# Splitting each chunk of feature weights into two halves, laid at two pairs of column offsets

## The chip, the cores and the metric

One core of one Trainium2 chip. The metric is the device time of one execution in microseconds (us). An execution on one core is measured a few times; the median is given. Beside it stands one execution taken with the profiler, from which all rows below come.

## The reference

One hybrid decoder layer on 256 tokens of width 1024, in float32:

```
u = rms_norm(h, attn_pre_norm);  q, k, v, x_lru, g_lru, gate_attn, gate_lru = split(u @ w_in)
attn   = causal attention, 8 heads of 128, rotary on 32 of the 128 dims of q and k
hl     = rg_lru(causal_conv4(x_lru));  r, i = sigmoid(block-diagonal 4 x (256 x 256))
merged = sigmoid(gate_attn) * (attn @ w_branch_attn) + sigmoid(gate_lru) * ((hl * gelu(g_lru)) @ w_branch_lru)
h = h + rms_norm(merged @ w_out)
h = h + rms_norm(relu(rms_norm(h) @ w_up)^2 @ w_down)
```

Seven products of 1024 x 1024 make `u @ w_in`, three more the branches and the output, four each the two parts of the feed-forward network.

## The kernel before

**Weights.** The weights are cut into 74 chunks of 128 x 2048 float32 (1 MB), numbered in the order of use: 0, 2, 4, 6 x_lru; 1, 3, 5, 7 v; 8 to 11 q; 12 to 15 k; 16 and 17 the gates of the recurrence (`rg`); 18 to 21 g_lru; 22 to 25 gate_attn; 26 to 29 gate_lru; 30 to 37 the branches; 38 to 41 the output; 42 to 57 up; 58 to 73 down. TensorE multiplies in fp32r, and a chunk is split in two for it: `hi` is the raw chunk cast to fp32r, and `lo` is raw minus `hi`. The activations are split alike (`xh`, `xl`), and a product is three matmuls (`three`, L179 to L182): hi·xh, hi·xl, lo·xh.

**Stages of a chunk.** SP loads the raw chunk (L92) into one of three buffers; ACT casts `hi` (L117), or DVE does for chunks 17 to 22 (L115, `HI_ON_VECTOR`); DVE subtracts `lo` (L118). `hi` and `lo` have three buffers each. `ahead(c)` issues the loads up to chunk c + 3 and the splits up to chunk c + 1 ahead of what follows it in the code; a split is issued at high priority, and a scheduler that goes by priorities then lays down the final order on each engine. The load of chunk c + 3 waits for the subtract of chunk c, since it takes its raw buffer; the cast of chunk c + 3 waits until PE has done with chunk c.

**A feature chunk.** In `feat_chunk` (L201) the output comes out as features on partitions, tokens on columns. A chunk holds 256 output features, as two halves o of 128, over 1024 inputs in eight blocks kb. PE goes through o, then kb, with three matmuls each, 48 in all; the stationary operand is a block of 128 x 128 of the weights, the moving one the activations of 128 x 256. In the chunk the columns lie as (kb, o, 128): the blocks that follow each other on PE are 256 columns apart. The two `rg` chunks (L337 on) use the same weights' layout, by groups g. The tiles of `hi` and `lo` are 64 columns wider than a chunk, and `OFFSET` shifts what lies in them, by c mod 3: `hi` and `lo` begin at columns (13, 16), (16, 13) or (13, 13). Chunk 0 has its own loop (`first_chunk`). The chunks of v, of the output (38 to 41), 42 and 43, and those of down go through other code, have no offsets and aren't touched.

**The rotation of the keys.** For chunks 12 to 15 DVE multiplies the sums by `rstd` into `kT` (L325), and POOL copies 32 rows of each chunk's result to `rot` by DMA (L326). Then DVE shuffles (L327), multiplies twice (L328, L329) and adds (L330), and POOL writes the 32 rows back into `kT` with four DMAs (L332). The scores of head 0, `s0` (L387, L388), read `kT`. The recurrence's product `it` (L361) runs on DVE in between.

Of the kernel before, what the change touches and what calls it, by code (L numbers as in the profile page):

```python
# [9 lines left out]
F32 = mybir.dt.float32  # L10
F32R = mybir.dt.float32r
AF = mybir.ActivationFunctionType
ALU = mybir.AluOpType
PSUM = bass.MemoryType.PSUM

P = 128
T = 256
D = 1024
KB = D // P
# [9 lines left out]
NCHUNK = 74  # L29


HI_ON_VECTOR = {c: 1.0 for c in range(17, 23)}


(P_W0, P_W1, P_W2, P_W3, P_CB, P_BA, P_BI, P_LAM, P_G1, P_G2) = range(0, 80, 8)
# [6 lines left out]

OFFSET = {c: ((13, 16), (16, 13), (13, 13))[c % 3] for c in (*range(0, 8, 2), *range(8, 38), *range(44, 58))}


@with_exitstack
def hybrid_layer(ctx: ExitStack, tc: tile.TileContext, head_d, x_d, w_d, cst_d, gp_d, out_d):
    nc = tc.nc  # L50
# [18 lines left out]
    def slot_tile(i, name, dt=F32, shape=(P, KB, T)):  # L69
        if i not in laid:  # L70
            laid.add(i)
            gap(slot, f"s{i}")
        return slot.tile(list(shape), dt, tag=f"s{i}", name=name)

    def mm_bank(name):
        return ps_mm.tile([P, 512], F32, tag="mm", name=name)
# [9 lines left out]
    raws, splits = {}, {}  # L86
# [8 lines left out]
    def weight_tiles(c):  # L95
        hi = whi_p.tile([P, 2048 + W_STEP], F32R, tag="whi", name=f"whi{c}")
        lo = wlo_p.tile([P, 2048 + W_STEP], F32R, tag="wlo", name=f"wlo{c}")
        h, l = OFFSET.get(c, (0, 0))
        return hi[:, h:h + 2048], lo[:, l:l + 2048]


# [2 lines left out]
    def split(c):  # L104
        raw, parts = raws.pop(c)
        if c in own_slots:
            hi, lo = (slot_tile(i, f"w{c}_{i}", F32R, (P, 2048)) for i in own_slots[c])
        else:
            hi, lo = weight_tiles(c)
        n = 2048 // parts  # L110
        for i in range(parts):
            s = slice(i * n, (i + 1) * n)
            k = i * n + int(n * HI_ON_VECTOR.get(c, 0))
            if k > i * n:
                nc.vector.tensor_copy(hi[:, i * n:k], raw[:, i * n:k])  # L115
            if k < (i + 1) * n:
                nc.scalar.copy(hi[:, k:(i + 1) * n], raw[:, k:(i + 1) * n])  # L117
            nc.vector.tensor_tensor(lo[:, s], raw[:, s], hi[:, s].bitcast(F32), ALU.subtract)  # L118
        splits[c] = (hi, lo)

    state = {"load": 0, "split": 0}
# [1 line left out]
    def ahead(c):  # L123

        while state["load"] < min(NCHUNK, c + 4):
            load(state["load"])
            state["load"] += 1
        while state["split"] < min(NCHUNK, c + 2):
            with tc.high_priority():
                split(state["split"])  # L130
            state["split"] += 1
# [47 lines left out]
    def three(out, wh, wl, xh, xl, start, stop):  # L179
        nc.tensor.matmul(out, wh, xh, start=start, stop=False)  # L180
        nc.tensor.matmul(out, wh, xl, start=False, stop=False)  # L181
        nc.tensor.matmul(out, wl, xh, start=False, stop=stop)  # L182

    def blocks(w):

        return w.rearrange("p (k o c) -> p k o c", k=KB, o=2)

    def of(x):
        return lambda kb: x[:, kb, :]

# [10 lines left out]
    def feat_chunk(c, xh, xl, urgent=False):  # L201

        ahead(c + 1)
        hi, lo = (blocks(w) for w in splits.pop(c))
        bank = mm_bank(f"mm{c}").rearrange("p (o t) -> p o t", o=2)
        for o in range(2):
            for kb in range(KB):
                three(bank[:, o, :], hi[:, kb, o, :], lo[:, kb, o, :], xh(kb), xl(kb),
                      kb == 0, kb == KB - 1)
        if not urgent:  # L210
            ahead(c + 2)
        return bank
# [51 lines left out]
    for j in range(4):  # L264
        s = slice(2 * j, 2 * j + 2)
# [71 lines left out]
    for c, dst, pb in ((C_RGA, rt, P_BA), (C_RGI, it, P_BI)):  # L337
        ahead(c + 1)
        hi, lo = splits.pop(c)
        hi = hi.rearrange("p (g k c) -> p g k c", g=4, k=2)  # L340
        lo = lo.rearrange("p (g k c) -> p g k c", g=4, k=2)
        for g in range(4):
            bank = mm_bank(f"rg{c}_{g}").rearrange("p (o t) -> p o t", o=2)
            for o in range(2):
                s = slice(o * P, (o + 1) * P)
                for k in range(2):
                    three(bank[:, o, :], hi[:, g, k, s], lo[:, g, k, s],
                          xch[:, 2 * g + k, :], xcl[:, 2 * g + k, :], k == 0, k == 1)
            for o in range(2):
                nc.scalar.activation(dst[:, 2 * g + o, :], bank[:, o, :], AF.Sigmoid,  # L350
                                     bias=pcol(pb, 2 * g + o))
# [83 lines left out]
    for kind, c0 in (("gL", C_GL), ("gA", C_GA), ("gelu", C_GEL)):  # L435
        for j in range(4):
            bank = feat_chunk(c0 + j, of(xgh), of(xgl))
            s = slice(2 * j, 2 * j + 2)
# [4 lines left out]
            else:  # L443
                g = tmp.tile([P, 2, T], F32, tag="g", name="g")
# [181 lines left out]
    for j in range(14):  # L626
        bank = feat_chunk(C_UP + j, lambda kb: u2h(kb, slice(0, T)), lambda kb: u2l(kb, slice(0, T)), True)
        o = 4 + 2 * j
# [4 lines left out]
        s = slice(o % 8, o % 8 + 2)  # L633
        hi = rrh[o // 8][:, s, :]
# [5 lines left out]
    parts = (halves, halves)  # L640
    norms = [TokenNorm("d", len(parts[b])) for b in range(2)]
    res = slot.tile([P, 2, D], F32, tag="s11", name="res")
    for b, i, acc in tok_products(C_DN, 16, lambda kb: (rrh[kb // 8][:, kb % 8, :], rrl[kb // 8][:, kb % 8, :]),
# [3 lines left out]
        s = parts[b][i]  # L647
# [7 lines left out]
def _rotary(np):  # L655

    inv = np.float32(500000.0) ** (-np.arange(0, 32, 2, dtype=np.float32) / np.float32(32))
    ang = (np.arange(T, dtype=np.float32)[:, None] * inv[None, :].astype(np.float32)).T
    cos = np.concatenate([np.cos(ang)] * 2)
    sin = np.concatenate([-np.sin(ang), np.sin(ang)])  # L660
    return np.tile(np.stack([cos, sin], axis=1), (4, 1, 1)).astype(np.float32)


def _pack(np, inp):

    def a(name):
        return np.asarray(inp[name])[0]

    def stat(w):
        k, n = w.shape  # L670
        w = w.reshape(k // P, P, n // 256, 256).transpose(2, 1, 0, 3)
        return [w.reshape(n // 256, P, 2048)]

    w_in = a("w_in")

    def halves(w):
        n = w.shape[1] // 512
        return w.reshape(2, 4, P, n, 512).transpose(3, 0, 2, 1, 4).reshape(2 * n, P, 2048)
# [12 lines left out]
    chunks += stat(w_in[:, 0:D])
    chunks += stat(w_in[:, D:2 * D])
    chunks += [rg(a("w_rg_a")), rg(a("w_rg_i"))]
    chunks += stat(w_in[:, 6 * D:7 * D])
    chunks += stat(w_in[:, 5 * D:6 * D])
    chunks += stat(w_in[:, 4 * D:5 * D])
    chunks += stat(a("w_branch_attn"))
    chunks += stat(a("w_branch_lru"))
    chunks += [mov(a("w_out"))]
    chunks += [halves(a("w_mlp_up")[:, 0:512])]  # L700
    chunks += stat(a("w_mlp_up")[:, 512:])
    chunks += [mov(a("w_mlp_down"))]
    w = np.concatenate(chunks, axis=0)
    w0, w = w[0].reshape(P, KB, 256), w[1:]

    rows = list(a("conv_w")) + [a(n) for n in ("conv_b", "b_rg_a", "b_rg_i", "lru_lambda",
                                               "attn_pre_norm", "mlp_pre_norm")]
    par = np.stack(rows).reshape(10, KB, P).transpose(2, 0, 1).reshape(P, NPAR)
    x = a("x")
    xw = np.concatenate([x.T.reshape(KB, P, T).transpose(1, 0, 2), w0], axis=2).reshape(P, KB * 512)  # L710
    return {
        "head": np.concatenate([par, xw], axis=1),
        "x": x,
        "w": w,
        "cst": _rotary(np),
        "gp": np.stack([a("attn_post_norm"), a("mlp_post_norm")]),
    }
# [19 lines left out]
```

## Time and profile before

| | us |
|---|---|
| runs | 437.81, 438.69, 438.76 (median 438.69) |
| the profiled execution | 438.56 |
| its span, first to last instruction | 436.8 |
| PE busy (matmuls) | 424.4 (97%) |
| DVE busy | 292.4 (67%) |
| ACT busy | 238.5 (55%) |
| share of PE in the chain that ended last | 91% |

The span is 1.8 us shorter than the profiled execution's time. Busy time of PE is that of overlapping matmuls: each is shown with its own length, 0.28 us for 256 columns, while the next starts 0.11 us after it. So how fast PE works is read from the starts of matmuls, not from their lengths, and whether it waits from the idle time ahead of one.

### The profile page before, as it was taken

The page shows a single profiled execution, that of the slowest core. Times are in us where ns is not written, and L with a number is a line of the kernel's source. Part 1 is how long each engine was busy: PE and PEld are TensorE (multiplying, and loading weights), DVE is VectorE, ACT ScalarE, POOL GpSimd, SP SyncE. Part 2 cuts the span into 40 slices and gives each one's busy share as a digit, 9 for nine tenths or more (in the row PEclk, how much of TensorE's full clock was granted, in tenths as well). Part 3 has the DMA queues.
Part 4 walks back from the last instruction along what each step waited for, and adds up shares of the span by engine and source line. Part 5 has one row for each costly group of instructions (what it writes and reads, how often), then busy time and mean ns, then how long its engine had stood idle before and what let it go on. Part 6 is the DMA issues. An engine that isn't in the chain of part 4 may idle for free.

```text
span 436.8 us, 7246 instructions
## 1 busy us (share of the span) xinstructions
PE 424.4 (97%) x3044; PEld 397.6 (91%) x3044; DVE 292.4 (67%) x353; ACT 238.5 (55%) x326; POOL 21.0 (5%) x48
## 2 busy tenths in 40 slices
PE   6989999999999999999999999999999999999994
PEld 6979999999999999999998879999999888888883
DVE  5649975779998646996689565666666644444434
ACT  7585663319996676663556474555555533333321
POOL 1000054202100000000000000000000000000000
PEclk9999999999999999999999999999999999999999
DMA  8969555665644355555567703455555555555102
GB/s 285 391 231 337 170 195 209 218 224 194 227 147 168 122 194 197 189 194 194 192 206 294 272 0 131 169 196 195 203 185 192 193 193 195 191 197 190 83 2 96
DMA packets 14576, 83.61 MB, mean 191 GB/s; under 512 B 1808, under 2 KB 2576, under 8 KB 5456
## 3 DMA queue, kind: packets, MB, share of 16 engines
q1 hardware_dynamic: 13520, 80.39, 50.8%
q0 software_dynamic: 736, 2.36, 1.7%
q8 instruction: 24, 0.39, 0.4%
q10 hardware_dynamic: 288, 0.39, 0.3%
q14 instruction: 8, 0.07, 0.0%
HBM read 81.04 MB, written 1.05 MB: 188 GB/s over the span
## 4 chain that ended last, share of the span: by engine, by line
PE 91%; DMA 5%; ACT 1%; DVE 1%; issue 0%; SPq 0%; DVEq 0%
PE mm L182 18%; PE mm L180 18%; PE mm L181 18%; PE acc L497 8%; PE acc L496 8%; PE acc L495 8%; DMA x_tok<-in_x_dram 3%; DMA wraw<-in_w_dram 1%; DMA xw_a<-in_head_dram 1%; PE up L602 1%; PE up L604 1%; PE rg L182 1%; PE v L234 1%; PE v L233 1%; PE up L603 1%; PE v L235 1%
## 5 line engine op out<-in xcount | busy, mean ns | idle before, releaser
L118 DVE TENSOR_TENSOR wlo<-wraw,whi 128x2048 fp32r<-128x2048 f32 (+2 forms) x78 | 163.5, 2100 | 84.7 <-ACT whi L117 84.7
L117 ACT CAST whi<-wraw 128x2048 fp32r<-128x2048 f32 (+2 forms) x72 | 125.2, 1741 | 90.9 <-PE acc L497 46.2
L180 PE MATMUL mm<-xgh,whi 128*128 128x256 f32 x384 | 108.2, 285 | 4.2 <-ACT xgh L171 4.2
L182 PE MATMUL mm<-xgh,wlo 128*128 128x256 f32 x384 | 107.1, 280 | 1.6 <-DVE wlo L118 1.6
L181 PE MATMUL mm<-xgl,whi 128*128 128x256 f32 x384 | 107.3, 280 | 0.0
L180 PEld LDWEIGHTS mm<-xgh,whi 128*128 128x128 f32 x384 | 72.4, 190 | 4.5 <-ACT xgh L171 4.2
L182 PEld LDWEIGHTS mm<-xgh,wlo 128*128 128x128 f32 x384 | 73.0, 190 | 1.8 <-DVE wlo L118 1.8
L181 PEld LDWEIGHTS mm<-xgl,whi 128*128 128x128 f32 x384 | 72.9, 190 | 0.5
L180 PE MATMUL mm<-u,whi 128*128 128x256 f32 x224 | 62.0, 277 | 0.0
L182 PE MATMUL mm<-u,wlo 128*128 128x256 f32 x224 | 62.0, 277 | 0.0
L181 PE MATMUL mm<-u,whi 128*128 128x256 f32 x224 | 62.0, 277 | 0.0
L495 PE MATMUL acc<-whi,rrh 128*128 128x512 f32 x128 | 49.8, 389 | 0.0
L496 PE MATMUL acc<-wlo,rrh 128*128 128x512 f32 x128 | 49.8, 389 | 0.0
L497 PE MATMUL acc<-whi,rrl 128*128 128x512 f32 x128 | 49.8, 389 | 0.0
L180 PEld LDWEIGHTS mm<-u,whi 128*128 128x128 f32 x224 | 42.1, 188 | 0.0
L181 PEld LDWEIGHTS mm<-u,whi 128*128 128x128 f32 x224 | 42.1, 188 | 0.0
L182 PEld LDWEIGHTS mm<-u,wlo 128*128 128x128 f32 x224 | 42.1, 188 | 0.0
L495 PEld LDWEIGHTS acc<-whi,rrh 128*128 128x128 f32 x128 | 24.0, 188 | 5.0
L496 PEld LDWEIGHTS acc<-wlo,rrh 128*128 128x128 f32 x128 | 24.0, 188 | 5.0
L497 PEld LDWEIGHTS acc<-whi,rrl 128*128 128x128 f32 x128 | 24.0, 188 | 4.9
L637 ACT CAST rrh<-rv 128x512 fp32r<-128x512 f32 x14 | 8.7, 621 | 34.7 <-DVE rv L636 34.7
L182 PE MATMUL mm<-lrh,wlo 128*128 128x256 f32 x64 | 17.7, 276 | 0.0
(197 smaller groups left out, 667.1 us busy)
## 6 DMA issues: line engine op xcount, KB each, us to landing
wraw<-in_w_dram SPq DMA_DIRECT2D x70, 1024.0 KB, 4.8
wraw<-in_w_dram SPq DMA_DIRECT2D x8, 256.0 KB, 5.8
xw_a<-in_head_dram SPq DMA_DIRECT2D x4, 256.0 KB, 4.5
wraw<-in_w_dram SPq DMA_DIRECT2D x2, 512.0 KB, 7.5
x_tok<-in_x_dram SPq DMA_DIRECT2D x1, 1024.0 KB, 11.3
gp<-in_gp_dram POOLq DMA_DIRECT2D x1, 1024.0 KB, 7.0
xw_b<-in_head_dram SPq DMA_DIRECT2D x3, 256.0 KB, 5.1
out_dram<-res ACTq DMA_DIRECT2D x2, 192.0 KB, 2.0
```

The costliest lines, as they stand in the source:

```text
L117: nc.scalar.copy(hi[:, k:(i + 1) * n], raw[:, k:(i + 1) * n])
L118: nc.vector.tensor_tensor(lo[:, s], raw[:, s], hi[:, s].bitcast(F32), ALU.subtract)
L180: nc.tensor.matmul(out, wh, xh, start=start, stop=False)
L181: nc.tensor.matmul(out, wh, xl, start=False, stop=False)
L182: nc.tensor.matmul(out, wl, xh, start=False, stop=stop)
L233: nc.tensor.matmul(banks[b], xgh[:, kb, s], hi[:, k, :], start=kb == 0, stop=False)
L234: nc.tensor.matmul(banks[b], xgh[:, kb, s], lo[:, k, :], start=False, stop=False)
L235: nc.tensor.matmul(banks[b], xgl[:, kb, s], hi[:, k, :], start=False, stop=kb == KB - 1)
L495: nc.tensor.matmul(out, xh[:, s], hi[:, hs], start=first, stop=False)
L496: nc.tensor.matmul(out, xh[:, s], lo[:, hs], start=False, stop=False)
L497: nc.tensor.matmul(out, xl[:, s], hi[:, hs], start=False, stop=last)
L637: nc.scalar.copy(hi, v)
```

## The change

The host lays out a chunk of features as (o, kb, 128) instead of (kb, o, 128), so that each half o is 1024 columns in one piece, and its blocks are 128 columns apart. In the tile the two halves are placed separately: `hi` at columns 13 and 1040, `lo` at 1040 and 13. Against the start of 1024 columns these are the pairs (13, 16) and (16, 13) for `hi` and `lo` of half 0 and half 1, though half 0 of `lo` lies in the upper part of its tile. Each half of a feature chunk is cast and subtracted by itself, 128 x 1024, and PE waits for each by itself. This holds for the `rg` chunks too. Chunk 0 has the offsets (13, 13) instead of (13, 16). Sizes and places of the tiles are as before.

```
+FEATURES = {*range(2, 8, 2), *range(8, 38), *range(44, 58)}
+HALF = 1024
+PLACE_HI = (13, HALF + 16)
+PLACE_LO = (HALF + 16, 13)
...
-        h, l = OFFSET.get(c, (0, 0))
+        if c in FEATURES:
+            return tuple([w[:, at:at + HALF] for at in places] for w, places in ((hi, PLACE_HI), (lo, PLACE_LO)))
+        h, l = (PLACE_HI[0], PLACE_LO[1]) if c == 0 else (0, 0)
         return hi[:, h:h + 2048], lo[:, l:l + 2048]
...
+        if c in FEATURES:
+            parts = max(parts, 2)
         n = 2048 // parts
         for i in range(parts):
...
+            r, s, h, l = raw[:, i * n:(i + 1) * n], slice(i * n, (i + 1) * n), hi, lo
+            if c in FEATURES:
+                s = slice(i * n % HALF, i * n % HALF + n)
+                h, l = hi[i * n // HALF], lo[i * n // HALF]
+            if c in HI_ON_VECTOR:
+                nc.vector.tensor_copy(h[:, s], r)
+            else:
+                nc.scalar.copy(h[:, s], r)
+            nc.vector.tensor_tensor(l[:, s], r, h[:, s].bitcast(F32), ALU.subtract)
...
         for o in range(2):
             for kb in range(KB):
-                three(bank[:, o, :], hi[:, kb, o, :], lo[:, kb, o, :], xh(kb), xl(kb),
-                      kb == 0, kb == KB - 1)
+                s = slice(kb * P, (kb + 1) * P)
+                three(bank[:, o, :], hi[o][:, s], lo[o][:, s], xh(kb), xl(kb), kb == 0, kb == KB - 1)
...
-        w = w.reshape(k // P, P, n // 256, 256).transpose(2, 1, 0, 3)
+        w = w.reshape(k // P, P, n // 256, 2, P).transpose(2, 1, 3, 0, 4)
```

The lines move: L117 and L118 become L126 and L127, L115 becomes L124, L180 to L182 become L189 to L191, the rotation's L325 to L332 become L330 to L337, the scores' L387 and L388 become L391 and L392, and `it`'s L361 becomes L365.

The scheduler's order moves with it, at three places that matter here. The numbers at the ends of names are those of buffers, and the number behind `whi`, `wlo`, `wraw` and `mm` is the chunk's.

The first is DVE around chunk 4. Before:

```order
L118 TENSOR_TENSOR wlo3_243<-wraw3_108,whi3_242 128x1024 x2
L253 RECIPROCAL rstd_t_361<-rstd_t_361 128x2
L118 TENSOR_TENSOR wlo4_275<-wraw4_218,whi4_274 128x2048
L259 COPY rstd_367<-bc_364 128x256
L270 TENSOR_TENSOR xlp_159<-mm0_0_168,rstd_367 128x256
L270 TENSOR_TENSOR xlp_159<-mm0_1_169,rstd_367 128x256
L118 TENSOR_TENSOR wlo5_330<-wraw5_220,whi5_329 128x2048
L277 SCALAR_TENSOR_TENSOR xc_161<-xlp_159,head_87,xc_161 128x256 x2
```

The same place of DVE after:

```order
L127 TENSOR_TENSOR wlo3_243<-wraw3_108,whi3_242 128x1024 x2
L258 RECIPROCAL rstd_t_363<-rstd_t_363 128x2
L127 TENSOR_TENSOR wlo4_275<-wraw4_218,whi4_274 128x1024 x2
L264 COPY rstd_369<-bc_366 128x256
L275 TENSOR_TENSOR xlp_159<-mm0_0_168,rstd_369 128x256
L275 TENSOR_TENSOR xlp_159<-mm0_1_169,rstd_369 128x256
L277 TENSOR_TENSOR xlp_159<-mm2_280,rstd_369 128x2x256
L127 TENSOR_TENSOR wlo5_332<-wraw5_220,whi5_331 128x2048
```

Chunk 4's subtract is in two pieces, and the product of chunk 2's sums into `xlp` has moved ahead of chunk 5's subtract.

The second is DVE at the rotation of the keys. Before:

```order
L118 TENSOR_TENSOR wlo18_1093<-wraw18_976,whi18_1092 128x2048
L327 STREAM_SHUFFLE rot_626<-rot_626 128x512
L328 TENSOR_TENSOR rot_626<-rot_626 128x512
L115 CAST whi19_1170<-wraw19_1033 128x2048
L329 TENSOR_TENSOR rot_626<-rot_626 128x512
L118 TENSOR_TENSOR wlo19_1171<-wraw19_1033,whi19_1170 128x2048
L330 TENSOR_TENSOR rot_626<-rot_626 128x512
L361 TENSOR_TENSOR it_1107<-it_1107,xc_161 128x1024
L115 CAST whi20_1244<-wraw20_1090 128x2048
L361 TENSOR_TENSOR it_1107<-it_1107,xc_161 128x1024
L118 TENSOR_TENSOR wlo20_1245<-wraw20_1090,whi20_1244 128x2048
```

The same place of DVE after:

```order
L127 TENSOR_TENSOR wlo18_1117<-wraw18_996,whi18_1116 128x1024 x2
L330 TENSOR_TENSOR kT_633<-mm15_1065,rstd_369 128x512
L124 CAST whi19_1196<-wraw19_1055 128x1024 x2
L127 TENSOR_TENSOR wlo19_1197<-wraw19_1055,whi19_1196 128x1024 x2
L332 STREAM_SHUFFLE rot_634<-rot_634 128x512
L333 TENSOR_TENSOR rot_634<-rot_634 128x512
L334 TENSOR_TENSOR rot_634<-rot_634 128x512
L365 TENSOR_TENSOR it_1133<-it_1133,xc_161 128x1024
L124 CAST whi20_1272<-wraw20_1114 128x1024 x2
L127 TENSOR_TENSOR wlo20_1273<-wraw20_1114,whi20_1272 128x1024 x2
L335 TENSOR_TENSOR rot_634<-rot_634 128x512
L365 TENSOR_TENSOR it_1133<-it_1133,xc_161 128x1024
```

The shuffle and both products have moved behind chunk 19's cast and subtract, and the add that ends the rotation has moved behind `it`'s product and chunk 20's cast and subtract.

The third is PE where chunk 18's matmuls (`mm18`) end and chunk 19's (`mm19`) begin. Before:

```order
L181 MATMUL mm18_1248<-xgl_124,whi18_1092 128x256
L182 MATMUL mm18_1248<-xgh_123,wlo18_1093 128x256
L387 MATMUL s0_1314<-kT_625,qT_624 128x128
L388 MATMUL s0_1314<-kT_625,qT_624 128x256
L180 MATMUL mm19_1328<-xgh_123,whi19_1170 128x256
```

After, some rows into chunk 19:

```order
L191 MATMUL mm19_1360<-xgh_123,wlo19_1197 128x256
L189 MATMUL mm19_1360<-xgh_123,whi19_1196 128x256
L391 MATMUL s0_1346<-kT_633,qT_632 128x128
L392 MATMUL s0_1346<-kT_633,qT_632 128x256
L190 MATMUL mm19_1360<-xgl_124,whi19_1196 128x256
L191 MATMUL mm19_1360<-xgh_123,wlo19_1197 128x256
```

The scores of head 0 have moved from the end of chunk 18 to behind the sixteenth of chunk 19's 48 matmuls. ACT's and SP's orders stay, but for the halves.

## Rows read from the trace of the kernel before

**Rows 1.** From the page: granted TensorE clock, span in 40 slices, tenths.

```profile
PEclk9999999999999999999999999999999999999999
```

**Rows 2.** Waits: who waited for whom; us, times, longest.

```profile
PE mm L182 <- DVE wlo L118: 1.6, 1, 1.6
```

**Rows 3.** Timeline, 26.3 to 31.2: start, us, engine, line, operation, [idle before <-releaser].

```profile
26.53 1.89 ACT L117 CAST whi<-wraw 128x2048 fp32r<-128x2048 f32 x1
28.45 2.29 DVE L118 TENSOR_TENSOR wlo<-wraw,whi 128x2048 fp32r<-128x2048 f32 x1 [1.63 <-ACT whi L117]
...
28.89 0.28 PE L181 MATMUL mm<-xgl,whi 128*128 128x256 f32 x1
29.47 1.89 ACT L117 CAST whi<-wraw 128x2048 fp32r<-128x2048 f32 x1
...
30.80 0.39 PE L182 MATMUL mm<-xgh,wlo 128*128 128x256 f32 x1 [1.62 <-DVE wlo L118]
```

**Rows 4.** Instructions by line and shape: busy us, mean ns, idle before.

```profile
L118 DVE TENSOR_TENSOR wlo<-wraw,whi 128x1024 fp32r<-128x1024 f32 x2 | 2.4, 1226 | 1.1 <-ACT whi L117 1.1
L117 ACT CAST whi<-wraw 128x1024 fp32r<-128x1024 f32 x2 | 2.1, 1052 | 0.9 <-DVE wlo L118 0.7
```

**Rows 5.** Timeline: chunk 6's subtract and its first matmul.

```profile
34.78 2.28 DVE L118 TENSOR_TENSOR wlo<-wraw,whi 128x2048 fp32r<-128x2048 f32 x1
...
41.62 0.28 PE L180 MATMUL mm<-xgh,whi 128*128 128x256 f32 x1
```

**Rows 6.** Timeline of PE: where q8, q9, q11, k12, up44 and its successor start.

```profile
52.73 0.28 PE L180 MATMUL mm<-xgh,whi 128*128 128x256 f32 x1
...
58.49 0.28 PE L180 MATMUL mm<-xgh,whi 128*128 128x256 f32 x1
...
69.60 0.28 PE L180 MATMUL mm<-xgh,whi 128*128 128x256 f32 x1
...
75.04 0.28 PE L180 MATMUL mm<-xgh,whi 128*128 128x256 f32 x1
...
266.04 0.28 PE L180 MATMUL mm<-u,whi 128*128 128x256 f32 x1
...
271.80 0.27 PE L613 MATMUL upT<-ident,upt 128*128 128x128 f32 x1
```

**Rows 7.** Timeline of DVE, 101 to 108 us: the rotation of the keys.

```profile
101.10 0.74 DVE L327 STREAM_SHUFFLE rot<-rot 128x512 f32<-128x512 f32 x1
...
102.48 1.22 DVE L115 CAST whi<-wraw 128x2048 fp32r<-128x2048 f32 x1
103.62 0.68 DVE L329 TENSOR_TENSOR rot<-rot 128x512 f32<-128x512 f32 x1
104.22 2.28 DVE L118 TENSOR_TENSOR wlo<-wraw,whi 128x2048 fp32r<-128x2048 f32 x1
106.42 0.68 DVE L330 TENSOR_TENSOR rot<-rot 128x512 f32<-128x512 f32 x1
107.38 1.23 DVE L361 TENSOR_TENSOR it<-it,xc 128x1024 f32<-128x1024 f32 x1 [0.28 <-ACT it L350]
```

**Rows 8.** DMA issues (count, KB, us to landing), POOL's and PE's timelines there.

```profile
wraw<-in_w_dram SPq DMA_DIRECT2D x1, 1024.0 KB, 5.3
kT<-rot POOLq DMA_DIRECT2D x1, 64.0 KB, 4.7
rot<-kT POOLq DMA_DIRECT2D x1, 64.0 KB, 1.9
107.40 0.50 POOL L332 DMA_DIRECT2D kT<-rot  x1 [7.89 <-DVE rot L330]
113.12 0.38 PE L387 MATMUL s<-kT,qT 128*128 128x128 f32 x2
```

**Rows 9.** Timeline of PE from its first matmul.

```profile
4.18 0.80 PE L180 MATMUL mm<-xgh,whi 128*128 128x256 f32 x2 [4.18 <-ACT xgh L171]
...
7.76 0.40 PE L182 MATMUL mm<-xgh,wlo 128*128 128x256 f32 x1
7.97 0.31 PE L181 MATMUL mm<-xgl,whi 128*128 128x256 f32 x1
```

More of the change, by code (lines that the diff above doesn't have):

```diff
@@ L29 @@
 NCHUNK = 74
-HI_ON_VECTOR = {c: 1.0 for c in range(17, 23)}
+HI_ON_VECTOR = range(17, 23)
 (P_W0, P_W1, P_W2, P_W3, P_CB, P_BA, P_BI, P_LAM, P_G1, P_G2) = range(0, 80, 8)
@@ L41 @@
 W_STEP = 64
-OFFSET = {c: ((13, 16), (16, 13), (13, 13))[c % 3] for c in (*range(0, 8, 2), *range(8, 38), *range(44, 58))}
+FEATURES = {*range(2, 8, 2), *range(8, 38), *range(44, 58)}
+HALF = 1024
+PLACE_HI = (13, HALF + 16)
+PLACE_LO = (HALF + 16, 13)
 @with_exitstack
@@ L109, in split @@
             hi, lo = weight_tiles(c)
+        if c in FEATURES:
+            parts = max(parts, 2)
         n = 2048 // parts
         for i in range(parts):
[L112 to L118, printed above, removed]
+            r, s, h, l = raw[:, i * n:(i + 1) * n], slice(i * n, (i + 1) * n), hi, lo
[7 more added lines that the diff above has]
+            nc.vector.tensor_tensor(l[:, s], r, h[:, s].bitcast(F32), ALU.subtract)
         splits[c] = (hi, lo)
@@ L182, in three @@
         nc.tensor.matmul(out, wl, xh, start=False, stop=stop)
-    def blocks(w):
-        return w.rearrange("p (k o c) -> p k o c", k=KB, o=2)
     def of(x):
@@ L203, in feat_chunk @@
         ahead(c + 1)
-        hi, lo = (blocks(w) for w in splits.pop(c))
+        hi, lo = splits.pop(c)
         bank = mm_bank(f"mm{c}").rearrange("p (o t) -> p o t", o=2)
@@ L339, in hybrid_layer @@
         hi, lo = splits.pop(c)
-        hi = hi.rearrange("p (g k c) -> p g k c", g=4, k=2)
-        lo = lo.rearrange("p (g k c) -> p g k c", g=4, k=2)
         for g in range(4):
@@ L344, in hybrid_layer @@
             for o in range(2):
-                s = slice(o * P, (o + 1) * P)
                 for k in range(2):
-                    three(bank[:, o, :], hi[:, g, k, s], lo[:, g, k, s],
+                    at = 512 * (g % 2) + 256 * k + P * o
+                    s = slice(at, at + P)
+                    three(bank[:, o, :], hi[g // 2][:, s], lo[g // 2][:, s],
                           xch[:, 2 * g + k, :], xcl[:, 2 * g + k, :], k == 0, k == 1)
@@ L703, in _pack @@
     w = np.concatenate(chunks, axis=0)
-    w0, w = w[0].reshape(P, KB, 256), w[1:]
+    w0, w = w[0].reshape(P, 2, KB, P).transpose(0, 2, 1, 3).reshape(P, KB, 256), w[1:]
     rows = list(a("conv_w")) + [a(n) for n in ("conv_b", "b_rg_a", "b_rg_i", "lru_lambda",
```

## The prediction

> **What bounds the kernel now.** I read first the page's table by slices, then the list of waits, then the order of the work around the one wait that it shows. TensorE is granted its full clock in every slice [rows 1], and PE is busy in 424.4 us of the span of 436.8 us (table above), so a microsecond is won or lost only where PE waits or where its matmuls follow each other more slowly. After the first chunk the list of waits holds one wait of PE for a split: 1.6 us at L182 [rows 2]. Everything that DVE and ACT do beside it is hidden. So there are three questions: what becomes of that wait, how fast do matmuls follow each other, and does the new order of instructions make PE wait elsewhere?
>
> **Term 1, the wait at chunk 4: a gain of 1.8 us.** The cast of chunk 4's weights starts at 26.53 and takes 1.89 us, the subtract starts at 28.45 and takes 2.29 us, so `lo` is there at 30.74; PE did its last matmul at 28.89 and goes on at 30.80 [rows 3]. After the change, the first half is cast in about 1.05 us and subtracted in about 1.23 us: both sizes stand in the trace [rows 4]. 26.53 + 1.05 + 0.03 + 1.23 = 28.84, and PE goes on some 0.06 us later, at 28.90; its own place for this matmul is 28.89 + 0.11 = 29.00. The wait is gone: 30.80 − 29.00 = 1.8 us. The second half's cast ends at about 28.65 and its subtract at about 30.1; PE reaches that half at 28.7 + 24 × 0.113 = 31.4, so it is in time. What is late next is chunk 5's `lo`: its cast starts at 29.47 [rows 3] and ends at 31.4, one added row of DVE (the `xlp` product, now ahead of it) and 2.3 us of subtract bring it to about 33.9, and PE, running 1.8 us earlier, wants it at about 34.5. That is a margin of 0.6 us; if it fails by as much, 0.6 us of the gain is lost. Bounds: 1.2 to 1.9.
>
> **Term 2, the added instructions: 0.** A split in halves costs 2 × 1.226 − 2.29 = 0.16 us more of DVE and 2 × 1.052 − 1.89 = 0.21 us more of ACT [rows 3, 4], over some 45 chunks at most 7 us of DVE and 10 us of ACT. What hides them is the lead of the splits: chunk 6's subtract starts at 34.78 and ends at 37.06, and PE starts chunk 6 at 41.62 [rows 5], a lead of 4.6 us; that no other chunk's split is waited for [rows 2] says the same of the rest. If this cover were gone, each chunk would cost 0.2 us.
>
> **Term 3, the columns: a gain of 0.6 us.** Forty-eight matmuls of a feature chunk take 75.04 − 69.60 = 5.44 us, 113 ns each, in most chunks; but chunk q8 takes 58.49 − 52.73 = 5.76 us, 120 ns each, and up44 takes 271.80 − 266.04 = 5.76 us [rows 6]. They are the same instructions on tiles of the same shapes, and the slow chunks that I found stand right behind other work of PE (chunks of values, transposes, attention). By the time at which single matmuls start, a slow chunk whose offsets are (16, 13) mostly returns to 113 ns within ten matmuls (chunk q10), one with (13, 13) does not (up44), one with (13, 16) rarely. After the change every chunk has (13, 16) in its first half and (16, 13) in its second, with a step of 128 columns between its blocks where there were 256. So I expect that a slow start lasts half a chunk. The excess of q8 and up44 is 0.32 us each, that of chunks 6 and q9 about 0.2 each, and in the stage of attention about 0.7 us in all by the starts of its matmuls; half of the 1.05 outside attention and a little of the rest make 0.6 us. From below: that halves with (13, 16) keep more slow starts than (13, 13) and (16, 13) did, −0.3; from above: all of it but the first few matmuls, 1.4. The Trainium skill, "TensorE: Matmul & The Clock Gate" (Part 2, step ①), says that PE has two independent read ports and that loading the next weights takes no read bandwidth from the running matmul; by this the offsets would change nothing, and the sum would be 0.6 us higher. The trace does not agree so simply: two rates for one instruction, 5.44 and 5.76 us [rows 6].
>
> **Term 4, the first scores: a loss of 3.3 us.** This is a by-effect of the order, shown above for DVE and PE. The keys' rotation ends with an add (before L330, after L335), and a POOL DMA then writes the rotated rows into `kT`, which the scores of head 0 (`s0`) read. Before, this add stands right behind chunk 19's subtract. After, it stands behind the shuffle, both products, `it`'s product and both halves of chunk 20's cast and subtract. By the starts of [rows 7]: the cast of chunk 19 starts at 102.48 and takes 1.14 to its successor, the subtract 2.20 (104.22 to 106.42); a split in halves adds 0.1 to each, so chunk 19 is done at 102.48 + 1.2 + 2.3 = 105.98. Then shuffle 0.75, two products 0.6 each (103.62 to 104.22), `it` 1.2, cast 1.2, subtract 2.3: 112.6. (The shuffle may wait up to 0.5 us more for the last `rot<-kT` DMA, which is now queued behind a weight load.) Times of this clock are all early by the gains above, PE's and DVE's alike, since chunk 19's cast waits for PE to release a buffer; the difference stays.
>
> The subtract of chunk 20 releases the raw tile that weight load 23 waits for, so SP issues this 1 MB load at 112.6, and the add and POOL's DMA come about 1.6 us behind it. Before, the same pair stands one chunk earlier: the subtract of chunk 19 ends at 104.22 + 2.28 = 106.50, its load takes 5.3 us, POOL issues the first `kT` write at 107.40, and this takes 4.7 us, to 112.1, though it is 64 KB and though one of its size takes 1.9 us with no load in flight [rows 7, 8]. The small write lands with the end of the load, 5.6 us behind the subtract. After: 112.6 + 5.6 = 118.2.
>
> When does PE want it? Before, `s0` starts at 113.12 [rows 8], a microsecond after `kT` has landed, ahead of chunk 19. After, it stands behind 16 of chunk 19's 48 matmuls: 113.12 + 16 × 0.113 = 114.93. PE then waits 118.2 − 114.9 = 3.3 us. Behind it in PE's queue are the other 32 matmuls of chunk 19 and all that follows, so nothing fills the gap. Bounds, with 112.6 to 113.1 for the subtract and 5.1 to 5.6 for the landing: 2.7 to 3.8. After the wait I expect no second one: DVE and ACT run ahead in it.
>
> **Sum.** 438.56 (the profiled execution) − 1.8 − 0.6 + 3.3 = 439.46, say 439.5. The profiled execution is 0.13 us below the median of the three runs (438.69), which I don't correct for.
>
> **Rivals.**
> *B, the write overtakes the load.* If the 64 KB write shares the DMA engines with the load packet by packet, it lands 1.9 us after its issue, as it did without a load in flight [rows 8]: add 0.6, issue 1.0 after that, so 112.6 + 1.6 + 1.9 = 116.1, and the wait is 1.2 us; 438.56 − 2.4 + 1.2 = 437.4 (437.0 to 437.8). Against it: the write of [rows 8] took 4.7 us beside a load. The Trainium skill, "DMA: Bandwidth & Descriptors" (section "Issuing engines are not separate DMA queues"), says that DMAs of the sync and gpsimd engines run on the same engines and interleave, which is this case; no row here shows such an early landing beside a load.
> *C, PE starts slowly again after the new wait; slower.* PE was idle until its first matmul at 4.18, and until 7.97 its matmuls follow each other by 0.21 us [rows 9], twice the 0.113 us of later, though the granted clock reads full in that slice too [rows 1]: 3.8 us at half the rate, which costs 1.9 us. If 3.3 us of idling at `s0` had the same effect, the time would be 439.5 + 1.9 = 441.4. It decides only if the wait is as long as I say; behind the 1.6 us of waiting at chunk 4 the matmuls go on at the full rate.
> *D, the slow rhythm spreads; slower.* If the pairs (13, 16) and the step of 128 columns make all 46 feature chunks run at 118 ns, each costs 0.22 us and the time is 439.5 + 10 = 449; if a third does, 443. Against it: one chunk in three has (13, 16) today, and nearly all of those are fast.
> *E, no wait at `s0`.* If DVE comes through its queue some 3 us sooner than I add up, or the load is not issued ahead of the write, the wait is gone and the time is 438.56 − 1.8 − 1.4 = 435.4 to 436.2.
> *F, the columns change nothing.* Matmuls are slow after other work for a reason that the offsets don't touch; then term 3 is 0, with the other terms as they are: 438.56 − 1.8 + 3.3 = 440.1.
>
> **How the numbers follow.** My forecast has 0.48 (438.3 to 440.5 by the bounds of its terms taken together), F 0.10, B 0.15, E 0.10, C 0.10, D 0.07. The range leaves out E and D, and reaches from B's lower side to C's upper: 436.6 to 441.5. About 0.2% (0.88 us here) is what a measurement can tell from no change: below 437.81 lie E, most of B and a sliver of the forecast, 0.25; within it a little over half of the forecast and some of B and F, 0.32; above it the rest of the forecast, most of F, and C and D, 0.43.
>
> **What would show it.** In the trace of the changed kernel: no wait of PE for `lo` of chunk 4 (term 1), or one of under 0.2 us; a wait of 2.7 to 3.8 us at the first matmul of L391 for a POOL DMA of L337's kind into `kT` that took more than 4 us (term 4; 1 to 1.4 us says B, none says E); chunk q8 and up44 nearer to 5.6 than to 5.76 us (term 3; unchanged says F, more slow chunks say D); matmuls that follow each other by 0.2 us right behind `s0` say C. The forecast is wrong altogether if the wait at L391 is missing.

## The result and the profile after

The changed kernel takes 442.91 us (median of 4 runs, 442.49 to 444.04), the kernel before in the same set 438.25 us (4 runs, 437.39 to 438.76). The ratio is 1.0123, with a 95% interval of 1.0108 to 1.0138: slower by 1.2%, some 5 us. The prediction said 439.5 us, 436.6 to 441.5; the time lies above its range.

The page of the changed kernel shows a span of 441.1 us, and in its row of granted TensorE clock a dip in the eleventh slice, from 110 to 121 us, and one at the very end, where [rows 1] had full speed:

```profile
span 441.1 us, 7344 instructions
PEclk9999999999899999999999999999999999999998
```

In its list of waits (us in total, times, longest) PE waits once after the start. The wait for `lo` of [rows 2] is not in it; in its place stands one for the DMA that writes the rotated keys:

```profile
PE s L391 <- DMA kT<-rot: 4.2, 1, 4.2
```

The timelines there (start, us, engine, line, operation, [idle before <-releaser]) answer to [rows 7] and [rows 8]: first DVE, then SP's load 23 and POOL's first write into `kT`, then PE:

```profile
105.20 0.01 DVE L332 LOAD_MASK_SELECT rot<-rot  x1 [1.08 <-DMA rot<-kT]
105.22 0.76 DVE L332 STREAM_SHUFFLE rot<-rot 128x512 f32<-128x512 f32 x1
...
109.57 2.36 DVE L127 TENSOR_TENSOR wlo<-wraw,whi 128x1024 fp32r<-128x1024 f32 x2
111.84 0.69 DVE L335 TENSOR_TENSOR rot<-rot 128x512 f32<-128x512 f32 x1
...
111.95 0.33 SPq L95 DMA_DIRECT2D wraw<-in_w_dram  x1
112.81 0.50 POOL L337 DMA_DIRECT2D kT<-rot  x1 [12.75 <-DVE rot L335]
...
113.05 0.28 PE L189 MATMUL mm<-xgh,whi 128*128 128x256 f32 x1
117.49 0.79 PE L391 MATMUL s<-kT,qT 128*128 128x128 f32 x2 [4.17 <-DMA kT<-rot]
118.08 1.06 PE L392 MATMUL s<-kT,qT 128*128 128x256 f32 x2
118.58 0.78 PE L190 MATMUL mm<-xgl,whi 128*128 128x256 f32 x1
119.15 0.41 PE L191 MATMUL mm<-xgh,wlo 128*128 128x256 f32 x1
119.36 0.41 PE L189 MATMUL mm<-xgh,whi 128*128 128x256 f32 x1
...
120.81 0.28 PE L190 MATMUL mm<-xgl,whi 128*128 128x256 f32 x1
120.93 0.28 PE L191 MATMUL mm<-xgh,wlo 128*128 128x256 f32 x1
```

The chain can be read straight down. The subtract of chunk 20 ends at 109.57 + 2.36 = 111.93. Load 23 goes out at 111.95, the add ends at 112.5, and the write goes out at 112.81. By the table of DMA issues (count, KB, us to landing) the load takes 5.2 us and the write of a sixteenth of its size 4.6:

```profile
wraw<-in_w_dram SPq DMA_DIRECT2D x1, 1024.0 KB, 5.2
kT<-rot POOLq DMA_DIRECT2D x1, 64.0 KB, 4.6
```

PE starts its last matmul ahead of the wait at 113.05 and `s0` at 117.49. Then it works at half its rate: the matmuls at 119.15 and 119.36 are 0.21 us apart, those at 120.81 and 120.93 0.12 us. The table by stretches (us; busy time and count of PE, PEld, DVE, ACT, POOL; granted clock; DMA share; GB/s) shows the granted clock of the two stretches behind the wait at 0.58 and 0.56, the lower of TensorE's two levels (1.2 GHz of 2.4) for most of the time, after 4 us in which PE was busy for 0.32:

```profile
113.00:117.00 4.00, 0.32 (x3) 0.12 (x2) 4.00 (x5) 2.95 (x5) 2.94 (x4) 1.00 0.86 314
117.00:119.00 2.00, 1.51 (x5) 1.33 (x6) 0.73 (x2) 0.63 (x1) 0.00 (x0) 0.58 0.33 76
119.00:121.00 2.00, 2.00 (x12) 2.00 (x11) 1.82 (x7) 0.00 (x0) 0.00 (x0) 0.56 0.96 401
121.00:123.00 2.00, 2.00 (x19) 2.00 (x19) 1.16 (x2) 1.91 (x5) 0.00 (x0) 1.00 0.16 61
```

So the changed kernel showed the predicted wait, longer than predicted, and rival C behind it, both at once.

### The profile page after: what moved, and what is told of

Its sections match the earlier page's. It is cut to its first block, busy times and chain, and to the rows that moved or that the text cites. A ratio compares the mean times of both kernels' runs of the same rounds, so it can differ in the third digit from the quotient of the medians.

```text
span 441.1 us, 7344 instructions
## 1 busy us (share of the span) xinstructions
PE 425.9 (97%) x3044; PEld 398.4 (90%) x3044; DVE 296.8 (67%) x405; ACT 243.4 (55%) x366; POOL 21.1 (5%) x48
## 3 DMA queue, kind: packets, MB, share of 16 engines
q0 software_dynamic: 736, 2.36, 1.6%
## 4 chain that ended last, share of the span: by engine, by line
PE 86%; issue 5%; DMA 4%; DVE 3%; ACT 1%; SPq 1%; POOL 0%; DVEq 0%; POOLq 0%
PE mm L190 17%; PE mm L189 17%; PE mm L191 17%; PE acc L499 8%; PE acc L500 8%; PE acc L501 8%; PE v L238 2%; PE v L239 2%; PE v L240 2%; DMA xw_b<-in_head_dram 1%; DMA rot<-kT 1%; DMA kT<-rot 1%; PE up L606 1%; PE up L608 1%; PE s L392 1%
## 5 line engine op out<-in xcount | busy, mean ns | idle before, releaser
L127 DVE TENSOR_TENSOR wlo<-wraw,whi 128x1024 fp32r<-128x1024 f32 (+2 forms) x124 | 166.8, 1378 | 69.5 <-ACT whi L126 69.3
L126 ACT CAST whi<-wraw 128x1024 fp32r<-128x1024 f32 (+2 forms) x112 | 128.9, 1186 | 100.7 <-PE acc L501 46.7
L189 PE MATMUL mm<-xgh,whi 128*128 128x256 f32 x384 | 108.3, 286 | 4.3 <-ACT xgh L180 4.2
L191 PE MATMUL mm<-xgh,wlo 128*128 128x256 f32 x384 | 107.3, 280 | 0.0
L189 PEld LDWEIGHTS mm<-xgh,whi 128*128 128x128 f32 x384 | 72.7, 191 | 4.7 <-ACT xgh L180 4.5
L191 PEld LDWEIGHTS mm<-xgh,wlo 128*128 128x128 f32 x384 | 73.3, 191 | 0.1
L189 PE MATMUL mm<-u,whi 128*128 128x256 f32 x224 | 62.0, 277 | 0.0
L191 PE MATMUL mm<-u,wlo 128*128 128x256 f32 x224 | 61.9, 276 | 0.0
L189 PEld LDWEIGHTS mm<-u,whi 128*128 128x128 f32 x224 | 42.1, 188 | 0.0
L191 PEld LDWEIGHTS mm<-u,wlo 128*128 128x128 f32 x224 | 42.1, 188 | 0.0
L191 PE MATMUL mm<-lrh,wlo 128*128 128x256 f32 x64 | 17.7, 276 | 0.0
```

The lines of the kernel that those rows point to most:

```text
L126: nc.scalar.copy(h[:, s], r)
L127: nc.vector.tensor_tensor(l[:, s], r, h[:, s].bitcast(F32), ALU.subtract)
```

## The experiments

Two theories stood against each other. A: the whole loss lies at `s0`, as a wait of some 4.2 us, made by DVE's order and the load ahead of the write, and a slow restart of PE of some 1.8 us behind it; the rest of the change gains. B: the smaller casts and subtracts, or the columns, cost time by themselves. The kernel before ran beside each batch (437.49, 437.55 and 437.78 us); each ratio is to it.

**`late_rope`: the order alone, without the change.** The kernel before, with K's shuffle and products pinned behind chunk 19's subtract and the add behind chunk 20's:

```
+        def turn_end(dst, pin):
+            add = nc.vector.tensor_tensor(r1, r1, r2, ALU.add)
+            if pin:
+                tc.keep_in_program_order(add)
...
+    if c == C_RGI:
+        turn(True)
...
+            if c0 + j == C_GL:
+                ahead(C_GL + 1)
+                turn_end(kT, True)
             bank = feat_chunk(c0 + j, of(xgh), of(xgl))
```

(`turn` holds the shuffle, pinned likewise, and the two products.)

> The kernel before, whole chunks and its own offsets, with only DVE's order at the keys' rotation made late: shuffle and products behind chunk 19's subtract, the add behind it's two products and chunk 20's cast and subtract; the scheduler then puts s0 behind 24 of chunk 19's 48 matmuls. Theory A (that order alone costs the time): the subtract of chunk 20 ends at about 113.8, load 23 goes out ahead of the kT writes, these land 5.5 us behind, at 119.3, s0's place is 115.8: a wait of 3.5 us and a slow restart of 1.6 us, 438.25 + 5.1 = 443.4 us, 442.3 to 444. Theory B (the halves or the columns are needed for the loss): within 0.5 us of the kernel before.

Measured: 442.46 us, ratio 1.0107 (1.0090 to 1.0124), 5.0 us over before. The wait and the clock behind it:

```profile
PE s L398 <- DMA kT<-rot: 3.3, 1, 3.3
```

```profile
118.00:120.00 2.00, 1.66 (x9) 1.58 (x10) 0.62 (x5) 0.00 (x0) 0.00 (x0) 0.76 0.83 260
120.00:122.00 2.00, 2.00 (x11) 2.00 (x11) 2.00 (x5) 0.73 (x3) 0.00 (x0) 0.50 0.69 274
```

The order of the rotation on DVE (shuffle, products and add), and the place of `s0` that the scheduler derives from it, are enough for the loss; no half and no column is needed for it. Theory B falls as the cause.

**`rope_all`: the change, with the order put right.**

```
-        nc.vector.stream_shuffle(r2, r1, swap)
...
+        with tc.high_priority():
+            nc.vector.stream_shuffle(r2, r1, swap)
...
```

with the same around the products into `qT` and `kT`, the add and the DMAs.

> The changed kernel with the keys' and queries' rotation (the products into qT and kT, shuffle, products, add and POOL's DMAs) issued at high priority, so that DVE has the add that ends it between the two halves of chunk 19's subtract, and the scores s0 stand again at the end of chunk 18. Theory A (the whole loss lies at s0: a wait of about 4.2 us and a slow restart of PE of about 1.7 us behind it, and the halves and their columns gain about 2.5 us elsewhere): no wait at s0, 438.25 - 2.5 = 435.8 us, 435.2 to 436.5. Theory B (the added instructions or the columns cost time by themselves): it stays above 438.3. The kernel before on the same chip: about 438.3.

Measured: 436.63 us, ratio 0.9972 (0.9962 to 0.9983): faster than before, by 0.9 to 1.2 us and not by the 2.5 of theory A. PE doesn't wait after the start. So the loss was at `s0`, and more than half of the gain that I saw between the first two profiles is missing.

**`c4_halves`: term 1 alone.** The kernel before, chunk 4 cast and subtracted by output halves:

```
+        if c == C_XL + 4:
+            for o in range(2):
+                r, h, l = (blocks(w)[:, :, o, :] for w in (raw, hi, lo))
+                nc.scalar.copy(h, r)
+                nc.vector.tensor_tensor(l, r, h.bitcast(F32), ALU.subtract)
```

> The kernel before with one edit: chunk 4 alone is cast and subtracted in two halves, by output half, from the old layout (blocks of 128 columns out of each 256). DVE's order at the keys' rotation and s0's place are those of before. Term 1 of the prediction: the wait of 1.6 us at L182 goes, 438.25 - 1.8 = 436.45 us, 436.2 to 437.0. Rival: chunk 5's lo or a later load becomes late and takes it back, 438.0 to 438.5.

Measured: 437.32 us, ratio 0.9994 (0.9983 to 1.0005): nothing. It was the time that the rival gave, but not by its mechanism, since its trace has no wait behind chunk 4 either. That asked for the kernel before itself, once more.

**`before_again`: the kernel before, profiled a second time.**

> The kernel before, profiled once more. Theory X (the wait of 1.6 us at chunk 4 belonged to the one execution profiled first, in which x_tok landed at 22.66 us; the cast of chunk 4 stands behind ACT's squares of x_tok and starts 3.87 us after x_tok lands): x_tok lands at 21.1 to 21.6 as in the profiles of the other kernels, the cast starts at 25.0 to 25.5, and PE does not wait at L182. Theory 1 (as predicted): a wait of 1.4 to 1.8 us at L182 again.

Measured: 437.89 us, and no wait of PE after its first matmul. In the first profile of before `x_tok` took 11.3 us to land (DMA issue, then ACT's timeline):

```profile
x_tok<-in_x_dram SPq DMA_DIRECT2D x1, 1024.0 KB, 11.3
```

```profile
22.68 1.06 ACT L250 ACTIVATE junk<-x_tok 128x1024 f32<-128x1024 f32 x1 [3.04 <-DMA x_tok<-in_x_dram]
```

In the second, the same views, 9.1 us; below ACT's rows stands PE's second matmul of chunk 4:

```profile
x_tok<-in_x_dram SPq DMA_DIRECT2D x1, 1024.0 KB, 9.1
```

```profile
21.38 1.06 ACT L250 ACTIVATE junk<-x_tok 128x1024 f32<-128x1024 f32 x1 [1.49 <-DMA x_tok<-in_x_dram]
...
25.23 1.89 ACT L117 CAST whi<-wraw 128x2048 fp32r<-128x2048 f32 x1
...
30.17 0.28 PE L181 MATMUL mm<-xgl,whi 128*128 128x256 f32 x1
```

ACT squares `x_tok` before it casts chunk 4, so the cast starts 3.87 us after `x_tok` lands: at 26.53 in [rows 3], at 25.23 here. PE reached that matmul at 30.17 in the second profile and at 28.89 in [rows 3]. The cast 1.3 us earlier and PE 1.3 us later are together more than the 1.6 us of [rows 2]. PE came later because its slow start lasted longer: in [rows 9] its matmuls follow each other by 0.21 us until 8.0 us, in the second profile until 10.6, and chunk 0 took 8.66 us there instead of 7.46:

```profile
10.40 0.38 PE L182 MATMUL mm<-xgh,wlo 128*128 128x256 f32 x1
10.61 0.28 PE L181 MATMUL mm<-xgl,whi 128*128 128x256 f32 x1
```

In the twelve profiles of the changed kernel and of the other experiments ACT starts on `x_tok` at 21.0 to 22.0 us; in the first profile of before it does at 22.7. So the wait belonged to that one execution, in which `x_tok` came latest and PE was early. How often the two meet in other executions isn't known, but it can't be the rule: `c4_halves`, which splits this chunk, gains nothing in the time.

**`load_behind`: the load taken from ahead of the write.** The changed kernel, its late add included:

```
+        if c == 23:
+            note = small.tile([32, 8], F32, tag="note", name="note")
+            tc.keep_in_program_order(nc.sync.dma_start(note, kT[0:32, 0, 0:8]))
```

> The changed kernel with one edit on SP: ahead of weight load 23 a DMA of 1 KB that reads the first kT rows back, so that load 23 goes out only when the first kT write has landed. DVE's late add and s0's place (behind 16 matmuls of chunk 19) are those of the changed kernel. Theory A (the write lands late because the 1 MB load was issued ahead of it): it lands about 1.9 us after its issue instead of 4.6, the wait at s0 falls from 4.2 to about 1.5 us, too short for the slow restart, and the time by 2.7 + 1.7, to about 438.5 by the changed kernel's 442.9 (ratio to before 1.001, 0.998 to 1.004). Theory E (POOL's writes take 4 to 5 us at this place by themselves): ratio 1.012 as for the changed kernel.

Measured: 438.43 us, ratio 1.0022 (1.0006 to 1.0038), 4.4 us better than the changed kernel by the ratios. DMA issue, PE's timeline and the stretch behind the wait:

```profile
kT<-rot POOLq DMA_DIRECT2D x1, 64.0 KB, 1.8
```

```profile
114.55 0.49 PE L396 MATMUL s<-kT,qT 128*128 128x128 f32 x2 [1.35 <-DMA kT<-rot]
```

```profile
115.00:117.00 2.00, 2.00 (x18) 1.95 (x17) 2.00 (x3) 0.81 (x1) 0.79 (x2) 1.00 0.70 119
```

The same write at the same place lands in 1.8 us instead of 4.6 when no load is ahead of it, and the wait falls by 2.8 us. The clock doesn't fall behind it.

**`warm`: work for PE in the wait.** The changed kernel with nine matmuls ahead of `s0` whose sums are overwritten:

```
+            for _ in range(9):
+                tc.keep_in_program_order(
+                    nc.tensor.matmul(sb[:, 256:512], qT[:, 0, 0:128], qT[:, 1, :], start=True, stop=True))
...
```

(The rest of the edit pins `s0` behind the same sixteen matmuls of chunk 19.)

> The changed kernel with nine matmuls of 128x256 float32 put on PE right ahead of s0 (their sums are overwritten), which fill some 3.9 us of the wait with work; s0 stays behind the same 16 matmuls of chunk 19 and waits for the same kT write. Theory C (PE restarts slowly behind s0 because it idled for 4.2 us): kT lands at the same time, the matmuls behind s0 follow each other by 0.113 us instead of 0.213, and the time falls by 1.5 to 1.9 us, to about 441.2. Theory D (the slow restart comes from s0 itself or from the DMA traffic there): the pitch behind s0 stays at 0.21 us and the time at 442.9.

Measured: 442.87 us (440.62 to 443.15), ratio 1.0107 (1.0083 to 1.0131). The pitch is as theory C says: full rate and a full grant right behind `s0`, after a last idle time of 2.0 us (PE's timeline, then the stretch).

```profile
119.47 0.49 PE L401 MATMUL s<-kT,qT 128*128 128x128 f32 x2 [2.03 <-DMA kT<-rot]
...
120.35 0.28 PE L218 MATMUL mm<-xgh,wlo 128*128 128x256 f32 x1
120.47 0.28 PE L189 MATMUL mm<-xgh,whi 128*128 128x256 f32 x1
```

```profile
120.00:122.00 2.00, 2.00 (x18) 1.96 (x17) 1.65 (x6) 1.66 (x2) 0.00 (x0) 1.00 0.97 401
```

The time is not: in the profiled execution load 23 took 6.3 us instead of 5.2, the write 5.7 instead of 4.6, and it went out 0.9 us later, so `s0` started 2 us later than in the changed kernel and gave the gain back. The 0.9 us were there before the nine matmuls ran: the last `rot<-kT` DMA landed at 105.99 instead of 105.07. One of the four runs took 440.62 us, as theory C asks, the other three 442.69 to 443.15. So the cause of the slow restart is shown (idling, not `s0` and not the DMA traffic); its price in time is not shown by this run, but read off the trace.

**The columns.** Six kernels are `rope_all` with other places for the halves and nothing else changed but, in `old_offsets`, chunk 0's offsets. PE's order is the same in all of them, and so are the other engines' orders in all but `swap`. In `swap` the two halves overlap by three columns, whose weights are those of the second half, and the orders of DVE and ACT move with it; `swap2` has the same pairs without the overlap, in the order of `rope_all`.

```
 old_offsets   OFFSET of before, by chunk, both halves alike
 swap          PLACE_HI = (16, HALF + 13)    PLACE_LO = (HALF + 13, 16)
 swap2         PLACE_HI = (HALF + 16, 13)    PLACE_LO = (13, HALF + 16)
 zero          PLACE_HI = (0, HALF)          PLACE_LO = (0, HALF)
 even16        PLACE_HI = (16, HALF + 16)    PLACE_LO = (16, HALF + 16)
 all_16_13     PLACE_HI = (16, HALF + 16)    PLACE_LO = (13, HALF + 13)
```

> The kernel rope_all (the changed kernel with the rotation at high priority) with the offsets of before: (13, 16), (16, 13) or (13, 13) by chunk, both halves alike; halves, layout (128 columns from block to block) and order stay. Term 3: the slow rhythm again lasts whole chunks (2, q8, up44 at 5.76 us, ge28 at 5.74), 0.7 to 1.0 us over rope_all, ratio to before 0.999 to 1.001. Rival (the step of 128 columns made the gain, not the offsets): as rope_all, 0.997.

> The kernel rope_all with the two pairs exchanged: (16, 13) in the first half of each chunk, (13, 16) in the second. If a chunk with (16, 13) leaves the slow rhythm within ten matmuls, as q10 and c4 did before, the first halves that are slow in rope_all (2, 6, q8, gL21, ge29, up44 by 0.13 us, gA22 to ge26 by 0.06) lose most of that: 0.5 to 0.9 us under rope_all, ratio to before 0.9955. Rival: the second pair brings the rhythm in or the first keeps it to the end, as ge28 did: as rope_all or up to 1 us over it.

> The kernel rope_all with the two pairs exchanged, and no two halves over each other: lo's half 0 and hi's half 1 at column 13, the others at 1040, so (16, 13) in the first half of each chunk, (13, 16) in the second. Theory P (each pair has its own rhythms, whatever half it is in, and leaves them only after an idle moment or at random): as swap, ratio to before 0.997 to 0.9985, chunks gA22 to ge26 at 5.65 us and chunk 4, ge27 and ge28 at 5.7 to 5.9. Theory Q (the first 24 matmuls of a chunk with (16, 13) clear the rhythm): 0.5 us under rope_all, 0.996.

> The kernel rope_all with no offsets in the feature chunks: both halves of hi and lo at columns 0 and 1024. Theory P: a pair of equal offsets keeps the slow rhythm, as (13, 13) did in q8 and up44: each chunk behind an interruption takes 5.76 us to its end, 1.3 to 2 us over rope_all, ratio 1.000 to 1.002. Rival (any shift between hi and lo of the same place costs, and 0 is the best): under rope_all, 0.996.

> The kernel rope_all with the pair (16, 16) in both halves. Theory P: as zero. If 13 and not the difference between hi and lo makes the slow rhythm, chunks behind an interruption run at 113 ns: 1 us under rope_all, ratio 0.995.

> The kernel rope_all with the pair (16, 13) in both halves. Theory P: chunks behind an interruption either leave at once (5.44, 5.54 or 5.65 us in the attention) or stay at 117, 122, 114 ns to the end as ge28 did (5.74): between swap and before, ratio 0.997 to 1.000. Theory Q: as its first halves, 0.996.

Measured, with the time of the 45 feature chunks from the first matmul of each to the 48th's successor, summed over the trace (chunk 0 and the `rg` chunks left out):

| kernel | pairs (hi, lo) of half 0, half 1 | median us | ratio to before (95%) | 45 chunks, us |
|---|---|---|---|---|
| before (second profile) | by chunk, three pairs | | | 249.0 |
| `old_offsets` | the same | 437.49 | 0.9997 (0.9989 to 1.0006) | 249.0 |
| `rope_all` | (13, 16), (16, 13) | 436.63 | 0.9972 (0.9962 to 0.9983) | 248.2 |
| `swap` | (16, 13), (13, 16) | 436.80 | 0.9984 (0.9975 to 0.9992) | 248.4 |
| `swap2` | (16, 13), (13, 16) | 436.35 | 0.9960 (0.9944 to 0.9976) | 248.0 |
| `all_16_13` | (16, 13) throughout | 442.21 | 1.0096 (1.0077 to 1.0114) | 253.2 |
| `even16` | (16, 16) throughout | 442.84 | 1.0111 (1.0093 to 1.0128) | 253.8 |
| `zero` | (0, 0) throughout | 450.08 | 1.0276 (1.0255 to 1.0298) | 261.0 |

The sums follow the times: 12.0 us more in `zero` stand for 12.3 us more time, 4.8 in `even16` for 5.1, 4.2 in `all_16_13` for 4.4. PE's timelines, where chunks start, show how. First q8 and its successor in `old_offsets` (5.76 us), then in `rope_all` (5.57), then q10 and its successor in `zero` (5.75), where before had already come down to 5.46:

```profile
51.31 0.28 PE L191 MATMUL mm<-xgh,whi 128*128 128x256 f32 x1
...
57.07 0.28 PE L191 MATMUL mm<-xgh,whi 128*128 128x256 f32 x1
```

```profile
51.55 0.28 PE L189 MATMUL mm<-xgh,whi 128*128 128x256 f32 x1
...
57.12 0.28 PE L189 MATMUL mm<-xgh,whi 128*128 128x256 f32 x1
```

```profile
63.20 0.28 PE L189 MATMUL mm<-xgh,whi 128*128 128x256 f32 x1
...
68.95 0.28 PE L189 MATMUL mm<-xgh,whi 128*128 128x256 f32 x1
```

`old_offsets` takes chunk by chunk what before takes, though its blocks are 128 columns apart and not 256: the step and the halves cost nothing, the offsets make the gain. With one pair throughout, the slow rhythm goes on from chunk to chunk: 120 ns in all 45 chunks of `zero`, 118 ns from q8 to gL18 in `even16` and `all_16_13`, which run at 113 ns only in some other stretches. With a change between (13, 16) and (16, 13) inside each chunk the rhythm ends at the change, wherever no matmuls of the attention stand between: in `rope_all` a slow chunk is slow for 24 matmuls. Not every change of pair ends it: in `old_offsets` q9 with (13, 16), behind q8 with (13, 13), still takes 5.65 us, 118 ns in both halves, and q10 with (16, 13) comes down to 5.46. Theory P (each pair keeps its rhythm until something ends it) fits these three kernels, though I had expected the rhythm only behind interruptions and so 2 us in `zero`, not 13; what it lacked is that a change between these two pairs ends the rhythm. Theory Q (the first half with (16, 13) clears it) falls, since `all_16_13` keeps it; the ratio of `swap2`, 0.996 as Q gave it, has an interval that reaches P's range too. `swap` missed the 0.9955 that I expected and came where its rival had it. In `swap2` the second half is the fast one again in chunks 2, 6, q8 and up44, as in `rope_all`, and the attention's chunks gA22 to ge26 come at 5.65 us instead of 5.70. What in the addresses makes a rhythm, the runs don't say.

## Why the prediction was wrong

**The wait at `s0` (term 4): right in place and mechanism, too small.** The late add, the load issued ahead of the write, the write landing 5.5 us behind the subtract (5.6 predicted) and `s0`'s place were as worked out. The wait was 4.2 us, not 3.3, because the subtract of chunk 20 ended later: DVE idled 1.08 us at the shuffle for the last `rot<-kT` DMA. This was in the text as "up to 0.5 us more" and was left out of the value. That DMA is another small transfer behind a load: the product that writes chunk 15's keys into `kT` had moved behind chunk 18's subtract, and load 21 went out just ahead of the copy. It took 5.5 us, where [rows 8] has 1.9:

```profile
rot<-kT POOLq DMA_DIRECT2D x1, 64.0 KB, 5.5
```

The 1.9 us of [rows 8] were not, as the prediction reads them, those of a transfer with no load in flight: load 20 was issued 3.5 us ahead of it and landed 0.6 us before it. `load_behind` gives the time without a load, 1.8 us. It confirms the pricing of a write behind a load, and with it that rival B does not hold here. The Trainium skill, "DMA: Bandwidth & Descriptors" (section "Issuing engines are not separate DMA queues"), says that such DMAs run on the same engines and interleave; when a small transfer lands it does not tell there, and the trace's 4.6 against 1.8 us decides.

**The slow restart (rival C): given 0.10, and it happened.** This is the step that failed: the sum holds nothing for PE's restart behind the wait. Without its 1.8 us the time would be 441.1 us, inside the range. Taking away one of the two smaller misses instead, 0.9 us of the wait or some 1.1 us of term 1 (1.8 forecast, while the second profile of before, without the wait, has a span 0.7 shorter), leaves it outside. I set C beside the wait as a case of its own and held the absence of a slow start behind 1.6 us of waiting against it, though that wait was less than half as long as the one I forecast. From the start of `s0` to the end of chunk 19 the changed kernel takes 123.53 − 117.49 = 6.0 us; at full rate it would be 0.47 for the scores and 32 × 0.113, 4.1 us. So the restart costs 1.9 us, as C said. What C held against itself from the start of the kernel, that [rows 1] reads full speed there, was no evidence: the trace's records of the granted clock begin at 8.01 us, just where the slow matmuls of [rows 9] end, and at 10.60 us in the second profile, where they end there.

**The wait at chunk 4 (term 1): real in the trace, absent from the time.** The arithmetic was right for the profiled execution, but the wait hung on `x_tok`, which landed 1.3 us later there than in the second profile, and on PE's early start. Its own row could have raised the question: the cast's start was taken as given, and what released it was not followed back to a DMA. `c4_halves` puts its worth at 0.06% with an interval around zero.

**The columns (term 3): right.** 0.6 us was predicted, with up to 1.4. `rope_all` against `old_offsets`, which differ in the offsets alone, is 0.25% by the ratios, 1.1 us, and 0.8 us by the sum of the chunks. A slow start lasts half a chunk, as the prediction said, for a reason that it didn't give: the change between the two pairs, in either order, and not the pair (16, 13) itself. The sum of slow chunks left out chunk 2 (5.76 us before, 5.57 after). Rival E (no wait at `s0`), rival F (the columns change nothing) and rival D (the rhythm spreads) fall; D came true only in kernels that keep one pair throughout. The Trainium skill, "TensorE: Matmul & The Clock Gate" (Part 2, step ①), says that PE has two read ports and that loading the next weights takes no read bandwidth from the running matmul; that does not keep the place of the weights from mattering here: between `zero` and `swap2` lie 3.2%.

**The added instructions (term 2): right.** No wait for a split in any profile of a kernel with halves.

By the two profiles that can be compared, of the changed kernel and of `before_again`, the time adds up. Chunk 18 starts at 105.9 instead of 107.0 us, 1.1 earlier, of which 0.5 are the scatter of the start and 0.6 the rhythm; from there to chunk 20 it takes 18.1 instead of 12.1 us, 6.0 more: 4.2 of waiting and 1.8 of restart. The rest differs by 0.1, and the spans by 441.1 − 436.1 = 5.0.

## What to carry to other kernels

An edit that cuts instructions in pieces also moves others in a scheduler's order. Compare the orders and look for the small step, off the busiest engine, whose DMA feeds that engine; here a rotation whose add came behind a subtract cost 6 us, and issuing it at high priority gave a kernel faster than both (436.63 us, and 436.35 with the pairs exchanged, which the intervals don't tell apart). A wait that shows in one profile is a gain only if it is in the other executions too: follow it back, and if it ends at a DMA, profile again before pricing it. And where the forecast is a long wait of TensorE, its restart belongs to the price.

## What the runs showed of the hardware that was not expected

- Behind idle times of PE of 4.2 us (the changed kernel) and 3.3 us (`late_rope`) the granted clock fell to 0.56 and 0.50 in a stretch of 2 us, and matmuls of 256 columns followed each other by 0.213 us; behind 1.4 us (`load_behind`) and 2.0 us (`warm`) the grant stayed at 1.00.
- A write of 64 KB that is issued 0.9 us behind a load of 1 MB landed 0.2 to 0.3 us after the load, 4.6 us after its issue; with no load ahead it took 1.8 us.
- Back-to-back matmuls of 256 columns with 128 x 128 weights follow each other by 113 ns or, in the mean of a chunk, by 118 to 120 ns, by the columns at which the weights stand in their tiles. The slow rhythm, once begun behind other work of PE, goes on over many chunks where the columns stay (118 ns from q8 to gL18 in `even16`); it ended where they changed between (13, 16) and (16, 13), and not where they changed from (13, 13) to (13, 16). Weights at columns 0 and 1024 cost 13.5 us more than the two-pair layout.
